# Attention 0 of a two-layer encoder: the norm's squares on ScalarE, the guard read from the matmul's bank, norm factors and outputs issued later

## The chip, the cores and the metric

The kernel runs on one core of a Trainium2 chip. A core has TensorE (PE in the profile, with its weight loads as PEld), VectorE (DVE), ScalarE (ACT) and GpSimd (POOL), and SyncE (SP), which here issues the transfers. Each engine takes its instructions in one fixed order. The time is device microseconds of one execution. Three runs of the kernel before gave 1396.01, 1396.46 and 1397.87 us: the median is 1396.46.

## The reference

Two layers over 1024 tokens of width 1024, in float32. Layer 0 is differential attention with 8 heads; layer 1 is latent attention. What matters here is layer 0:

```python
q = _rope(q.reshape(b, s, 2 * DA_HEADS, DA_QK_DIM), positions)
k = _rope(k.reshape(b, s, 2 * DA_HEADS, DA_QK_DIM), positions)
...
sc = jnp.einsum('bqhcd,bkhcd->bhcqk', qb, k) * scale
p = jax.nn.softmax(sc, axis=-1)
p = p[:, :, 0] - lam * p[:, :, 1]
o = jnp.einsum('bhqk,bkhd->bqhd', p, v)
...
o = _rmsnorm(o, subln_g) * (1.0 - lambda_init)
o = o.reshape(b, s, DA_WIDTH) * jax.nn.silu(z)
return o @ w_out
```

Every head has two softmaxes; their difference multiplies the values, and each token's 128 outputs of a head are divided by their root mean square (plus 1e-6), multiplied by a gain and by a gate silu(z).

## The kernel before, in words

**Tiles.** Attention 0 goes head by head (8), each in 8 tiles of 128 queries, four tiles to a half head. `q_tile` (line 856) computes both score matrices of a tile (128 x 1024 each, matmuls L866), the two softmaxes without their division (L412 the maximum, L414 the exponential with its sum: the first sum goes into a column of `zz`), and combines them (L872 to L874). The sums of the first softmax are not divided out: the norm that follows removes any factor of a row, so only its small added constant needs them. One and two tiles later the combined matrix is transposed (L395), split into high and low parts (L397 on ScalarE, L398 on VectorE) and multiplied by the values (`pv`, L173 to L175).

**Between them** TensorE works on strips of the input projection for the next head (`stream0`, lines 272 and 312): k, q and z. Their results go through the rotation (`rope`, line 324: L331 or L333 on ScalarE, four transfers L335, L336, L341 and L343 on POOL) and are stacked into high and low operands: `stack_q` (line 361) has two copies on ScalarE (L364, L365), two subtractions on POOL (L366, L367), and four transfers (L369, L370) that fill the other halves of qa and qb. The scores of the next head read these.

**The norm of a half head.** When the last tile of a half has been multiplied, `close` (line 1027) calls `head_out` (L931 squares the output, L932 scales it) and `subln` (line 934), which multiplies by the gate on POOL (L938) and puts `rest` on the list `hooks`. `rest` (line 942) sums the squares over the 128 partitions with small matmuls (L945) into `pt`, four columns of a bank. Then `zz` is squared (L948), the small constant times that square is added to the sum (L949), the guard compares (L950: a row whose sum of squares is too large for float32 gets a factor of 0), the sum is limited (L951), POOL raises it to the power -0.5 (L169) and multiplies by the guard (L953). `finish` (line 902) writes the 512 factors to memory (L420), reads them back spread over all partitions (L422), multiplies the output by them on POOL (L908) and stores it (L912).

**Order.** `after_scores` (line 1008) copies the list `hooks` before the second half of `pv`, and runs the copied entries after it, in each tile. So a hook that puts another on the list runs one tile earlier than that one. In numbers of tiles within a head, the gate multiply L938 of the first half is in tile 5 and that of the second half in tile 1 of the next head; `rest` is in tiles 6 and 2.

Instructions are traced in this order, and a scheduler then orders each engine by a simulation: an instruction may be issued ahead of its place when its inputs are ready. Two things pin it. `in_turn` (line 184) puts an instruction behind the one traced before it on its engine; L938, L953, L908, the rotation's and the stacks' POOL instructions and most other POOL work are pinned so, L169 is not. `tc.keep_in_program_order` does the same for some transfers of the last head; `tc.issue_after` puts one instruction behind a given one.

**The last head** has its own parts: `rest` of its first half is run by `extra0` (line 1293), which also loads and splits operands of the output projection (L1198 on ScalarE, L1199 on POOL or VectorE) and starts that projection (`Pre7`). For this half `pt` is four columns of an accumulator of `Pre7`. `run_tails` (line 993) finishes the last two tiles, the hooks left are run, and the stored first half of head 7 is read back (line 1385). The second half of head 7 goes another way (`dst` is given): its factors are spread by matmuls (L922, L923).

Of the kernel before, what the change touches and what calls it, by code (L numbers as in the profile page):

```python
# [11 lines left out]
F32 = mybir.dt.float32  # L12
# [3 lines left out]
AF = mybir.ActivationFunctionType  # L16
ALU = mybir.AluOpType
# [4 lines left out]
P = 128  # L22
# [4 lines left out]
HF = 512  # L27
NH = 8
QL = 384
KVL = 256  # L30
EPS = 1e-6
# [38 lines left out]
GUARD = 2.0 ** 40  # L70
FMAX = 3.4028e38
# [5 lines left out]
def f32v(ap):  # L77
    return ap.bitcast(F32)
# [3 lines left out]
def trunk(ctx: ExitStack, tc: tile.TileContext, A, out):  # L82
    nc = tc.nc
    SP, PE, V, S, G = nc.sync, nc.tensor, nc.vector, nc.scalar, nc.gpsimd

    def pool(stack, name, bufs=1, side="left", space=None):
        kw = dict(name=name, bufs=bufs, reuse_waits="tile")
        if space is not None:
            kw["space"] = space
            if space == DRAM:  # L90
                kw.pop("reuse_waits")
        else:
            kw["side"] = side
        return stack.enter_context(tc.tile_pool(**kw))
# [21 lines left out]
    def bank(tag, name, shape=None):  # L116
        nonlocal turn
        if tag == "acc":
            turn += 1
            if (turn - 1) % (2 + NB.get("accx", 0)) < 2:  # L120
                return psa.tile([P, HF], F32, name=name, tag="acc", bufs=2)
            tag = "accx"
        return ps.tile(shape or [P, HF], F32, name=name, tag=tag, bufs=NB[tag])

    dr = pool(ctx, "dr", bufs=1, space=DRAM)
# [6 lines left out]
    oF = [dr.tile([NH, 2, P, HF], F32, name=f"oF{l}") for l in range(2)]  # L132
# [33 lines left out]
    def rsqrt(w, n):  # L166

        y = sm.tile([P, n], F32, name="rq_y")
        G.tensor_tensor(out=y, in0=w, in1=mhalf[:, :n], op=ALU.pow)  # L169
        return y  # L170
# [9 lines left out]
    def behind(eng):  # L180

        return tc.issue_after(mk[eng]) if eng in mk else nullcontext()

    def in_turn(ins):

        return tc.keep_in_program_order(ins) if mk else ins
# [230 lines left out]
    def bcast_rows(sp, y, tag, bufs):  # L417

        d_ = dr.tile([HF], F32, name="bc_d", tag="bcd", bufs=4)
        SP.dma_start(d_.rearrange("(p t) -> p t", p=P), y)  # L420
        b = sp.tile([P, HF], F32, name="bc_s", tag=tag, bufs=bufs)
        SP.dma_start(b, d_[None, :].to_broadcast([P, HF]))  # L422
        return b, b.rearrange("p (q t) -> p t q", t=4)

    def t3(ap_):
        return ap_.rearrange("p (t q) -> p t q", t=4)
# [173 lines left out]
    for f in range(2):  # L600
        fs = slice(f * HF, f * HF + HF)
        spread = PE.matmul(cb[:, fs], ones[0:1, :], crow[0:1, fs], start=True, stop=True).ins
# [298 lines left out]

    def finish(o, y, l, h, half, dst, ap_, dgs):

        if dst is None:
            b, rb = bcast_rows(ap_, y, "osq", 4)

            def scale():
                in_turn(G.tensor_mul(t3(o), t3(o), rb))  # L908
                hooks.append(lambda: hooks.append(store))

            def store():
                SP.dma_start(oF[l][h, half], o)  # L912

            if l == 0 and (h, half) >= (NH - 2, 1):
                hooks.append(lambda: hooks.append(scale))
            else:
                hooks.append(scale)
            return
        rb = bank("z", "rb") if l else Y[1]
        for j in range(4):  # L920
            js = slice(j * P, (j + 1) * P)
            S.mul(dgs[:, js], ident, y[:, j : j + 1])  # L922
            PE.matmul(rb[:, js], ones, dgs[:, js], start=True, stop=True)  # L923
        V.tensor_mul(o, o, rb)
# [9 lines left out]
    def subln(o, sq, zz, half, h, dst):  # L934


        if dst is None:
            in_turn(G.tensor_mul(o, o, GZ[h][half]))  # L938
        else:
            V.tensor_mul(o, o, GZ[h][half])  # L940

        def rest():
            pt = Y[0] if dst is not None else ssq_at[0] if ssq_at else bank("acc", "ssq")
            for j in range(4):
                PE.matmul(pt[:, j : j + 1], sq[:, j * P : (j + 1) * P], ones[:, 0:1], start=True, stop=True)  # L945
            w = sm.tile([P, 4], F32, name="sl_w")
            fin = sm.tile([P, 4], F32, name="sl_f")
            V.tensor_mul(fin, zz, zz)  # L948
            V.scalar_tensor_tensor(out=w, in0=fin, scalar=P * EPS / GUARD ** 2, in1=pt[:, 0:4], op0=ALU.mult, op1=ALU.add)  # L949
            V.scalar_tensor_tensor(out=fin, in0=fin, scalar=FMAX / GUARD ** 2, in1=w, op0=ALU.mult, op1=ALU.is_ge)  # L950
            V.tensor_scalar(w, w, 3.0e38, None, op0=ALU.min)  # L951
            y = rsqrt(w, 4)
            in_turn(G.tensor_mul(y, y, fin))  # L953
            if dst is not None:
                return lambda: finish(o, y, 0, h, half, dst, None, sq)
            finish(o, y, 0, h, half, None, a0b, sq)

        if dst is None:
            (hooks if h < NH - 1 else rests).append(rest)
        else:  # L960
            return rest()
# [29 lines left out]
    tails, hooks = [None, None], []  # L991
# [171 lines left out]
    class Seven:  # L1163
# [32 lines left out]
        def put(self, raw, hi, lo, eng):  # L1196
            with behind("S"):
                S.copy(hi, raw)  # L1198
            sub = eng.tensor_sub(lo, raw, f32v(hi))  # L1199
            if eng is G:  # L1200
                in_turn(sub)
                self.sub = sub.ins
# [204 lines left out]
    def strip1(i, wpool=None):  # L1407
        return load_strip([A["w_s1"][i, f] for f in range(2)], [4, 4], wpool)
# [377 lines left out]
    for h in range(2):  # L1786
        w = strip1(6 + h)
# [286 lines left out]
    def attn1(h, fills, extra=None, late=None):  # L2074
# [5 lines left out]
        def close(half, o_, zz):  # L2080
            if late and half == 1:
                ctx_["late"] = late(o_, zz, ctx_["gz"])
                return
            o = ap2.tile([P, HF], F32, name="o1", tag="o", bufs=2)
            V.scalar_tensor_tensor(out=o, in0=o_, scalar=0.5, in1=ctx_["gz"], op0=ALU.mult, op1=ALU.mult)
            V.reciprocal(zz, zz)
            finish(o, zz, 1, h, half, None, ap2, None)
# [188 lines left out]
    def scale(tt, y):  # L2276
        full, early = xs_[tt], tt // 4
        c1, c2_ = halves[early], halves[1 - early]

        def second():  # L2280
            V.scalar_tensor_tensor(out=full[:, c2_], in0=full[:, c2_], scalar=y, in1=fg[:, c2_], op0=ALU.mult, op1=ALU.mult)
            SP.dma_start(out[tt][:, c2_], full[:, c2_])

        def first_():
            S.mul(full[:, c1], full[:, c1], y)
            SP.dma_start(out[tt][:, c1], full[:, c1])

        if tt == NT - 2:
            held.extend((second, first_))
        else:  # L2290
            second()
            first_()
# [160 lines left out]
```

## Time and profile before

| | |
|---|---|
| median of three runs | 1396.46 us |
| the profiled execution's own time | 1394.95 us |
| its span | 1393.2 us |
| TensorE busy | 1367.5 us (98%) |
| VectorE busy | 928.3 us (67%) |
| GpSimd busy | 753.1 us (54%) |
| ScalarE busy | 740.9 us (53%) |
| attention 0 | about 140 to 690 us of the span |

Instructions are named by their line: L908 is line 908. A group's row gives the operation, the tile written and the tiles read, the shapes, the count, then busy time in us, the mean of one in ns, and the idle time of its engine just before with what ended it. A row of the timeline gives the start and the duration in us, and in brackets the idle time before it with its releaser. In the rows of waits stand who waited, for whom, the total in us, how often, and the longest. Matmuls overlap, so their rows in the timeline run longer than the step from one to the next.

### The profile page before, as it was taken

Reading aid. Unit: us, or ns where it says so; the run is one execution under the profiler, and the core shown is the slowest. Engines: PE = TensorE matmul, PEld = TensorE weight load, DVE = VectorE, ACT = ScalarE, POOL = GpSimd, SP = SyncE. Lnnn points to the kernel's source line nnn. Section 1 sums busy time; section 2 is a strip of 40 time slices with the busy share of each in tenths; the row PEclk is TensorE's granted clock in tenths of the full one; section 3 lists DMA queues with packets and bytes.
Section 4 is the critical chain, followed back from the end, with each engine's and each line's share of the span. In section 5 each row is a group of like instructions: output and inputs, shape, how many; then the busy total and the mean of one; then the engine's idle time right before and its main releaser. Section 6 shows DMA issues by size and latency. Waiting matters only on the chain.

```text
span 1393.2 us, 20695 instructions
## 1 busy us (share of the span) xinstructions
PE 1367.5 (98%) x7334; PEld 1144.7 (82%) x7334; DVE 928.3 (67%) x1313; ACT 740.9 (53%) x1339; POOL 753.1 (54%) x593
## 2 busy tenths in 40 slices
PE   9999999999999999999999999999999999999997
PEld 6788888888888887887887888888888888888886
DVE  7655777777666666668596976545656555555684
ACT  5532465656565555567648553335454544545554
POOL 5424374758686858575794233532141373834673
PEclk9999999999999999999999999999999999999999
DMA  9857644343444434526564246489443364667463
GB/s 342 263 177 244 201 110 141 100 144 105 149 127 144 128 121 122 151 61 212 182 219 167 68 137 212 137 282 286 125 105 119 102 201 136 193 221 215 145 245 121
DMA packets 149386, 232.06 MB, mean 167 GB/s; under 512 B 20641, under 2 KB 57633, under 8 KB 149282
## 3 DMA queue, kind: packets, MB, share of 16 engines
q1 hardware_dynamic: 149282, 230.74, 52.7%
q8 instruction: 58, 0.95, 0.3%
q14 instruction: 46, 0.38, 0.1%
HBM read 144.74 MB, written 61.81 MB: 148 GB/s over the span
## 4 chain that ended last, share of the span: by engine, by line
PE 79%; DVE 6%; DMA 5%; ACT 3%; POOL 3%; issue 2%; SPq 1%; POOLq 0%; ACTq 0%; DVEq 0%
PE s L2067 10%; PE acc L173 9%; PE acc L175 9%; PE acc L174 9%; PE tr L395 7%; PE s L866 7%; PE pv L173 4%; PE pv L174 4%; PE pv L175 4%; PE vps L173 2%; PE vps L174 1%; PE vps L175 1%; PE zacc L175 1%; PE zacc L173 1%; PE zacc L174 1%
## 5 line engine op out<-in xcount | busy, mean ns | idle before, releaser
L397 ACT CAST pth<-tr 128x512 fp32r<-128x512 f32 x256 | 150.3, 587 | 285.7 <-PE tr L395 280.8
L412 DVE TENSOR_REDUCE nm<-s 128x1 f32<-128x1024 f32 x192 | 233.8, 1218 | 79.8 <-PE s L866 70.9
L398 DVE TENSOR_TENSOR ptl<-tr,pth 128x512 fp32r<-128x512 f32 x256 | 176.1, 688 | 150.3 <-ACT pth L397 146.3
L219 POOL TENSOR_TENSOR wl<-wraw,wh 128x512 fp32r<-128x512 f32 (+2 forms) x77 | 98.8, 1284 | 208.4 <-ACT wh L218 176.3
L414 ACT ACTIVATE e<-s,nm 128x1024 f32<-128x1024 f32 x128 | 143.5, 1121 | 35.4 <-DVE nm L412 35.0
L395 PE MATMUL tr<-ident,e 128*128 128x128 f32 x1024 | 155.0, 273 | 4.1 <-DVE ptl L398 3.8
L395 PEld LDWEIGHTS tr<-ident,e 128*128 128x128 f32 x1024 | 120.7, 140 | 46.5 <-DVE ptl L398 24.1
L173 PE MATMUL acc<-h0h,wh 128*128 128x512 f32 x360 | 150.2, 417 | 0.0
L173 PE MATMUL pv<-pth,vt 128*128 128x256 f32 x512 | 147.5, 288 | 0.0
L174 PE MATMUL pv<-ptl,vt 128*128 128x256 f32 x512 | 145.6, 284 | 0.0
L175 PE MATMUL pv<-pth,vt 128*128 128x256 f32 x512 | 144.6, 282 | 0.0
L175 PE MATMUL acc<-h0h,wl 128*128 128x512 f32 x360 | 141.5, 393 | 0.0
L174 PE MATMUL acc<-h0l,wh 128*128 128x512 f32 x360 | 141.1, 392 | 0.0
L336 POOL TENSOR_TENSOR rp_r<-rp_raw,cosT 128x512 f32<-128x512 f32 x36 | 47.0, 1305 | 104.4 <-ACT rp_raw L333 52.9
L173 PEld LDWEIGHTS pv<-pth,vt 128*128 128x128 f32 x512 | 97.2, 190 | 2.9 <-ACT pth L397 0.2
L174 PEld LDWEIGHTS pv<-ptl,vt 128*128 128x128 f32 x512 | 97.4, 190 | 2.4
L175 PEld LDWEIGHTS pv<-pth,vt 128*128 128x128 f32 x512 | 97.3, 190 | 0.0
L1199 POOL TENSOR_TENSOR wol<-wol,woh 128x512 fp32r<-128x512 f32 x56 | 82.3, 1492 | 26.0 <-ACT woh L1198 24.4
L866 PE MATMUL s<-ks,qa 128*128 128x512 f32 x256 | 82.7, 403 | 4.4 <-DVE e L874 3.2
L874 DVE SCALAR_TENSOR_TENSOR e<-s,z,e 128x1024 f32<-128x1024 f32 x64 | 82.2, 1284 | 2.2
L866 PE MATMUL s<-ks,qb 128*128 128x512 f32 x256 | 79.8, 393 | 1.2 <-DMA qb<-qb 1.2
L175 PEld LDWEIGHTS acc<-h0h,wl 128*128 128x128 f32 x360 | 67.6, 188 | 15.1
(427 smaller groups left out, 3461.1 us busy)
## 6 DMA issues: line engine op xcount, KB each, us to landing
ada<-in_ada_ss SPq DMA_DIRECT2D x32, 512.0 KB, 5.9
wraw<-in_w_s SPq DMA_DIRECT2D x64, 256.0 KB, 2.8
vS<-v_hl SPq DMA_DIRECT2D x32, 512.0 KB, 5.9
vt<-vS SPq DMA_DIRECT2D x32, 512.0 KB, 4.9
wol<-tS SPq DMA_DIRECT2D x56, 256.0 KB, 5.2
tS<-ob SPq DMA_DIRECT2D x48, 256.0 KB, 2.0
rp_sw<-rp_raw SPq DMA_DIRECT2D x160, 64.0 KB, 2.0
bc_s<-bc_d SPq DMA_DIRECT2D x34, 256.0 KB, 4.2
```

What stands on the lines that cost most here:

```text
L173: PE.matmul(psum, ah, bh, start=first, stop=False, skip_group_check=skip)
L174: PE.matmul(psum, ah, bl, start=False, stop=False, skip_group_check=skip)
L175: mm3.last = PE.matmul(psum, al, bh, start=False, stop=last, skip_group_check=skip).ins
L219: sub = (V if pair_of else G).tensor_sub(l_[:, :n], raw[:, :n], f32v(h_[:, :n]))
L395: transpose_p.last = PE.transpose(tr[:, j, :], p[:, kt * P : (kt + 1) * P], ident).ins
L397: mk["S"] = S.copy(pth[kh][:, :, dst], tr).ins
L398: mk["V"] = V.tensor_sub(ptl[kh][:, :, dst], tr, f32v(pth[kh][:, :, dst])).ins
L412: mk["V"] = V.reduce_max(nm, s_ps, axis=AX.X, negate=True).ins
L414: mk["S"] = S.activation(e, s_ps, AF.Exp, bias=nm, scale=1.0, accum_out=zs).ins
L866: PE.matmul(s_ps[:, kc * HF : (kc + 1) * HF], src[:, c, ql], KS[h][kc][:, c, :], start=fst, stop=not fst)
L1199: sub = eng.tensor_sub(lo, raw, f32v(hi))
L2067: PE.matmul(s_ps[:, kc * HF : (kc + 1) * HF], lhs, rhs(kc), start=i == 0, stop=i == 4)
```

## The change

Three parts. The squares of `zz` are made by two ScalarE activations, one scaled for the small constant and one for the guard. VectorE then has two instructions instead of four: one limits the sum in the bank and adds the first square, the other compares the second square with the sum in the bank, which before was compared with the sum with its small constant. And `finish` for the halves of layer 0 that go through memory no longer issues the write, the read back, the multiply and the store from `rest` on, but each from a hook of its own: with `rest` in tile t, the write of the factors goes from t to t+1, the read back from t to t+2, the multiply from t+1 to t+3 (for the two late halves of heads 6 and 7 from t+2), the store from t+3 to t+4. The multiply stays pinned by `in_turn`. Layer 1 keeps its order.

```diff
     def finish(o, y, l, h, half, dst, ap_, dgs):
 
+        if dst is None and l == 0:
+            d_ = dr.tile([HF], F32, name="bc_d", tag="bcd", bufs=4)
+            rb = []
+
+            def put():
+                SP.dma_start(d_.rearrange("(p t) -> p t", p=P), y)
+                hooks.append(spread)
+
+            def spread():
+                b = ap_.tile([P, HF], F32, name="bc_s", tag="osq", bufs=4)
+                SP.dma_start(b, d_[None, :].to_broadcast([P, HF]))
+                rb.append(b.rearrange("p (q t) -> p t q", t=4))
+                hooks.append(scale)
+
+            def scale():
+                in_turn(G.tensor_mul(t3(o), t3(o), rb[0]))
+                hooks.append(store)
+
+            def store():
+                SP.dma_start(oF[l][h, half], o)
+
+            hooks.append(put)
+            return
         if dst is None:
             b, rb = bcast_rows(ap_, y, "osq", 4)
 
...
-            if l == 0 and (h, half) >= (NH - 2, 1):
-                hooks.append(lambda: hooks.append(scale))
-            else:
-                hooks.append(scale)
+            hooks.append(scale)
             return
...
-            V.tensor_mul(fin, zz, zz)
-            V.scalar_tensor_tensor(out=w, in0=fin, scalar=P * EPS / GUARD ** 2, in1=pt[:, 0:4], op0=ALU.mult, op1=ALU.add)
-            V.scalar_tensor_tensor(out=fin, in0=fin, scalar=FMAX / GUARD ** 2, in1=w, op0=ALU.mult, op1=ALU.is_ge)
-            V.tensor_scalar(w, w, 3.0e38, None, op0=ALU.min)
+            S.activation(w, zz, AF.Square, scale=math.sqrt(P * EPS) / GUARD)
+            S.activation(fin, zz, AF.Square, scale=1.0 / GUARD)
+            V.scalar_tensor_tensor(out=w, in0=pt[:, 0:4], scalar=3.0e38, in1=w, op0=ALU.min, op1=ALU.add)
+            V.scalar_tensor_tensor(out=fin, in0=fin, scalar=FMAX, in1=pt[:, 0:4], op0=ALU.mult, op1=ALU.is_ge)
             y = rsqrt(w, 4)
             in_turn(G.tensor_mul(y, y, fin))
```

## The prediction

> **What bounds the kernel now.** I read the page first, then the busy time by stretch, who TensorE waits for, and the instructions of each engine in order of time where TensorE waits.
>
> ```profile
> span 1393.2 us, 20695 instructions
> ```
> ```profile
> 140.00:400.00 260.00, 259.31 (x1435) 220.27 (x1434) 194.10 (x276) 152.90 (x271) 164.33 (x131) 1.00 0.45 132
> 400.00:690.00 290.00, 281.25 (x1586) 235.69 (x1586) 198.12 (x283) 171.46 (x303) 206.69 (x171) 1.00 0.45 136
> ```
>
> The two stretches are attention 0 (columns: length, then busy time of PE, PEld, DVE, ACT, POOL, then granted clock). TensorE is idle for 0.7 us in the first and 8.8 us in the second, at full clock. So the whole stage holds 9.5 us that any edit beside TensorE could win: 0.7% of the time. Losses have no such limit. What TensorE waited for there:
>
> ```profile
> PE s L866 <- DVE e L874: 3.2, 6, 1.0
> PE tr L395 <- DVE ptl L398: 2.8, 5, 0.9
> PE s L866 <- DMA qb<-qb: 1.2, 2, 0.7
> PE s L866 <- DMA qa<-qa: 0.9, 1, 0.9
> ```
>
> Two thirds of the idle time ends with VectorE, 2.1 us with the query operands qa and qb, which POOL (L366, L367) and SP deliver for the next head.
>
> **The change part by part.**
>
> *Vector arithmetic of the norm (16 half heads).*
>
> ```profile
> L948 DVE TENSOR_TENSOR sl_f<-zz 128x4 f32<-128x4 f32 x16 | 9.0, 565 | 0.0
> ...
> L950 DVE SCALAR_TENSOR_TENSOR sl_f<-sl_f,sl_w 128x4 f32<-128x4 f32 x16 | 6.6, 413 | 0.4
> L951 DVE TENSOR_SCALAR sl_w<-sl_w 128x4 f32<-128x4 f32 x16 | 6.0, 373 | 0.0
> ```
> ```profile
> L949 DVE SCALAR_TENSOR_TENSOR sl_w<-sl_f,ssq x14: 132/157/159, 195.8 to 640.9; 128x4 f32<-128x4 f32 x14
> ```
>
> L948 and L951 go. L949 stays with other operations; L950 now takes its second input from the matmul's bank, as L949 does, so I price it like L949: 157 ns in place of 413. VectorE sheds 9.0 + 6.0 + 16 x (0.413 - 0.157) = 19.1 us. Most of this lies under TensorE's work. Where it does not, the trace shows it:
>
> ```profile
> 331.72 1.22 DVE L951 TENSOR_SCALAR sl_w<-sl_w 128x4 f32<-128x4 f32 x1
> 332.85 0.26 DVE L873 TENSOR_SCALAR z<-z,zz,neglam 128x1 f32<-128x1 f32 x1
> 333.15 1.28 DVE L874 SCALAR_TENSOR_TENSOR e<-s,z,e 128x1024 f32<-128x1024 f32 x1
> ```
> ```profile
> 334.49 0.73 PE L866 MATMUL s<-ks,qa 128*128 128x512 f32 x2 [0.59 <-DVE e L874]
> ```
>
> L951 holds up the two steps behind it, L873 and L874, and TensorE waits 0.59 us for L874. Without L951's 1.22 us that wait is gone. Upper bound of the gain: all that VectorE ends, 3.2 + 2.8 = 6.0 us; lower bound: nothing, if other VectorE work fills the place. The wait above is the one I can tie to these instructions for certain; I take a quarter of the bound, **-1.5 us**, since most of the 11 waits end a chain of full-width softmax steps (L874's 1.28 us and its like) that stay.
>
> The bank is now read twice, the second time by the guard. In the last head it is an accumulator that TensorE overwrites later; the second read is 0.16 us, so nothing to at most 16 x 0.16 = 2.5 us. I take nothing, because no wait of TensorE on L949 is among the four above.
>
> *Two squares on ScalarE.* The trace has no Square of this shape. The nearest row is a small activation:
>
> ```profile
> L843 ACT ACTIVATE lp<-lp x1: 205/205/205, 105.1 to 105.1; 128x2 f32<-128x2 f32 x1
> ```
>
> 32 x 0.205 = 6.6 us, in 550 us where ScalarE is busy 152.90 + 171.46 = 324.4. The inputs are old by then, so the squares can go into gaps. In the worst case each stands ahead of a copy that TensorE wants: +6.6 us; in the best nothing. I take **+0.2**, near the idle end.
>
> [...] L948 took 565 ns on VectorE in the mean, L843 205 ns on ScalarE. [...]
>
> *The multiply by the norm factors (L908) goes two tiles later.* Put, spread and store go one, two and one tile later; but the trace shows that work which isn't pinned is issued when its inputs are there, not at its place in the text:
>
> ```profile
> 672.65 0.92 DVE L948 TENSOR_TENSOR sl_f<-zz 128x4 f32<-128x4 f32 x1
> ...
> 688.53 0.16 DVE L949 SCALAR_TENSOR_TENSOR sl_w<-sl_f,oy 128x4 f32<-128x4 f32 x1 [0.65 <-PE oy L945]
> ```
>
> These are neighbouring lines of one half head, 16 us apart. So I cost the two transfers, which are not pinned, at nothing: the same 15 of each on SP, behind the same producers (a gain or loss of one SP slot, 0.5 us, where they trade places with a query copy). L908 is pinned behind all earlier POOL work, so it does move: from tiles 3 and 7 of each head to tiles 5 and 1, and there it stands right behind L938, the gate multiply of the next half.
>
> ```profile
> L908 POOL TENSOR_TENSOR o<-o,bc_s 128x512 f32<-128x512 f32 x15 | 23.2, 1549 | 16.9 <-DMA bc_s<-bc_d 16.8
> ```
>
> What it gains: POOL's 16.8 us of waiting for the broadcast row end, as two more tiles pass. TensorE felt this once:
>
> ```profile
> 650.52 1.55 POOL L908 TENSOR_TENSOR o<-o,bc_s 128x512 f32<-128x512 f32 x1 [5.67 <-DMA bc_s<-bc_d]
> ```
> ```profile
> 654.48 0.50 PE L175 MATMUL oy<-woh,oal 128*128 128x512 f32 x1 [0.51 <-POOL oal L1199]
> ```
>
> That is **-0.5** (bounds 0 and -0.5). What it costs: 1.55 us of POOL at tile 5, ahead of the query operands of the next head. Head 4:
>
> ```profile
> 396.81 1.29 POOL L938 TENSOR_TENSOR o<-o,gz 128x512 f32<-128x512 f32 x1
> ...
> 405.77 1.29 POOL L366 TENSOR_TENSOR qb<-rp_r,qa 64x512 fp32r<-64x512 f32 x1
> 407.14 1.29 POOL L367 TENSOR_TENSOR qb<-rp_r,qa 64x512 fp32r<-64x512 f32 x1
> ```
> ```profile
> 411.22 0.47 PE L866 MATMUL s<-ks,qb 128*128 128x512 f32 x1 [0.55 <-DMA qb<-qb]
> ```
>
> POOL never pauses between these rows, and TensorE already waits: +1.55. Head 7 and head 3, with SP's copies of qb and the matmul that reads it:
>
> ```profile
> 603.24 1.28 POOL L938 TENSOR_TENSOR o<-o,gz 128x512 f32<-128x512 f32 x1 [4.07 <-ACT o L932]
> ...
> 616.28 1.29 POOL L367 TENSOR_TENSOR qb<-rp_r,qa 64x512 fp32r<-64x512 f32 x1
> ```
> ```profile
> 338.17 0.46 SPq L370 DMA_DIRECT2D qb<-qb x1
> 617.60 0.46 SPq L370 DMA_DIRECT2D qb<-qb x1
> ```
> ```profile
> 341.43 0.62 PE L866 MATMUL s<-ks,qb 128*128 128x512 f32 x2
> 620.37 0.62 PE L866 MATMUL s<-ks,qb 128*128 128x512 f32 x2
> ```
> ```profile
> DMA to landing us min/median/max: 2.2/2.3/5.7
> ```
>
> In head 7 POOL's pause of 4.07 us ends at L938, so nothing earlier helps. With 2.2 us to landing, head 7 has 620.37 - 619.8 = 0.6 us to spare and loses 1.0; head 3 has 341.43 - 340.4 = 1.0 and loses 0.5. In heads 5 and 6 the old place of L908 lies on the same unbroken stretch of POOL, so its going there pays for its coming:
>
> ```profile
> 518.07 1.57 POOL L908 TENSOR_TENSOR o<-o,bc_s 128x512 f32<-128x512 f32 x1
> ```
>
> I take 0 for these. Sum **+3.0**; bounds 0 and 5 x 1.55 = 7.75.
>
> *Last head.* L908 of head 6's second half comes behind the last L938 and ahead of a weight split that TensorE wants at once:
>
> ```profile
> 664.39 1.27 POOL L1199 TENSOR_TENSOR wol<-wol,woh 128x512 fp32r<-128x512 f32 x1
> ```
> ```profile
> 665.85 0.39 PE L174 MATMUL oy<-wol,oah 128*128 128x512 f32 x1
> ```
>
> It ends at 665.66, 0.19 us early, so 1.55 more makes up to 1.36 us of wait; I take **+1.0**, as VectorE paces what follows (bounds 0 and 1.4). The last L908 leaves its place before the splits and comes behind them; the store and reload of that row move some 4 us later on SP, where the loads behind them have over 8 us to spare. In the very last half, which the output projection waits for, POOL's power no longer follows L950 and L951, 0.41 + 0.37 us by their means: **-0.5**, as these steps are shorter where POOL is quiet; bounds 0 and -0.8.
>
> Sum: -1.5 + 0.2 - 0.5 + 3.0 + 1.0 - 0.5 = **+1.7 us**. The profiled execution took 1394.95 us, 1.75 outside its span; it becomes 1396.65. The median of the runs shown is 1.51 above it, so **1398.2 us**.
>
> **The rivals.**
>
> *POOL decides (slower).* L908 behind L938 delays the query operands of all five heads 3 to 7, 7.75 us, and the last head's split, 1.4; less 1.5, 0.5 and 0.5 that is +6.65, or 1403.1 us. It holds from the point where a head has less than 1.55 us to spare and POOL no pause between L938 and L367; three heads are shown to be so. Against it: in heads 5 and 6 L908 leaves the same stretch, and faster vector work lets POOL start earlier.
>
> *VectorE decides (faster).* If short vector work ends all its 6.0 us, and the two 0.5 with it, while L908 falls into pauses, the time is 1396.46 - 7.0 = 1389.5; half of this gives 1393.0. For it: the waits are VectorE's, by two thirds. Against it: L874, L412 and L398 stay as they are.
>
> *The squares decide (slower).* If each of the 32 stands ahead of a copy that TensorE wants, the term is 6.6 in place of 0.2, and the time 1404.6. For it: ScalarE's copies lie in TensorE's own loop. Against it: ScalarE has pauses for 41% of the stage, and the squares' inputs are two tiles old.
>
> *The moves don't take place in effect.* If POOL's order comes out as before, since what is pinned is pinned behind other work that itself waits, only the arithmetic counts: -1.5 + 0.2 - 0.5 = -1.8, or 1394.7 us.
>
> **How the numbers follow.** Forecast 0.32, POOL decides 0.29, the squares decide 0.03, VectorE decides 0.24, no moves in effect 0.12. About 0.2% (2.8 us) is what a measurement of this kernel tells from no change. The forecast and the third rival lie within it: 0.44. Slower 0.32, faster 0.24. The likeliest one's own range is 1394.5 to 1400.5. The range over all goes to 1391.5, where about a third of the faster case is left out, and to 1403, where the last part of the slower one is: about 0.16 outside.
>
> **What would show it.** Right: L908 directly behind L938 on POOL, with no wait for bc_s; L366 and L367 of heads 3, 4 and 7 later against the head's L938 by 1.5 us, and longer waits of the first score matmul of a head on qa and qb; the guard near 0.16 us in every half; the wait at 334.49 gone; squares of about 0.2 us on ScalarE. Wrong: waits on qa and qb no longer than now (then POOL has more room than I read), TensorE idle in attention 0 well under 8 us, or a new wait on pth behind the squares.

## The result, and the profile after

The changed kernel takes 1403.91 us (median of six runs, 1400.24 to 1405.51) where the kernel before takes 1396.36: a ratio of 1.0048, 95% interval 1.0032 to 1.0064. It is slower, by 7 us, and 0.9 us beyond the upper end of the range.

The profiled execution was the fastest of the six. Its own time is 1400.24 us. The first two rows of its page:

```profile
span 1398.5 us, 20660 instructions
...
PE 1366.8 (98%) x7334; PEld 1145.4 (82%) x7334; DVE 914.6 (65%) x1281; ACT 745.3 (53%) x1371; POOL 753.5 (54%) x593
```

VectorE is busy 13.7 us less than before (928.3), TensorE about as long as before (1367.5). The own times of the norm's instructions, four before and two now, fell by 19.2 us (24.1 to 4.9), as the prediction summed them; the busy time fell less: 6.1 us of the 24.1 overlapped neighbouring VectorE instructions before, and 2.8 of the 4.9 do now, which makes 3.3 of the 5.5 us between the two. The span grew by 5.3 us, so TensorE's idle time grew by 5.3 + 0.7 = 6.0 us. The two stretches of attention 0 (columns as in the prediction) hold 4.0 of these; another 2.0 lie ahead of 140 us, where TensorE's idle time ranges from 4.6 to 8.5 us over the profiles of all kernels here.

```profile
140.00:400.00 260.00, 260.00 (x1442) 221.40 (x1440) 188.22 (x263) 155.71 (x287) 166.92 (x133) 1.00 0.45 132
400.00:690.00 290.00, 276.56 (x1557) 232.37 (x1557) 187.55 (x262) 172.83 (x320) 198.77 (x165) 0.99 0.43 131
```

From 140 to 400 us TensorE has no idle time left: the wait at 334.49 is gone. From 400 to 690 us idle time has grown from 8.8 to 13.4 us. Whom TensorE waited for in attention 0 (140 to 700 us):

```profile
PE tr L395 <- DVE ptl L398: 7.8, 7, 2.6
PE s L866 <- DVE e L874: 1.9, 2, 1.2
PE oy L174 <- POOL wol L1219: 1.3, 1, 1.3
PE oy L173 <- ACT oah L1218: 1.1, 1, 1.1
PE oy L175 <- POOL oal L1219: 0.6, 1, 0.6
PE s L866 <- DMA qb<-qb: 0.3, 1, 0.3
```

The waits on qa and qb, which the prediction saw grow, have shrunk from 2.1 to 0.3 us. What has grown is the transpose's wait on ptl, from 2.8 to 7.8 us, and three waits in the last head are new. (Lines behind `finish` are 20 higher than before: L938 is now L958, L945 L965, L1199 L1219. L908 is now L919.)

**The stall ahead of head 5** (as in the prediction, a place is named by the head whose queries are being made) in the timeline of the changed kernel, engine by engine:

```profile
463.47 1.31 POOL L958 TENSOR_TENSOR o<-o,gz 128x512 f32<-128x512 f32 x1
464.71 1.56 POOL L919 TENSOR_TENSOR o<-o,bc_s 128x512 f32<-128x512 f32 x1
...
470.08 1.29 POOL L343 TENSOR_TENSOR rp_r<-rp_r,rp_sw 128x512 f32<-128x512 f32 x1
471.40 0.62 ACT L364 CAST qa<-rp_r 64x512 fp32r<-64x512 f32 x1 [3.81 <-POOL rp_r L343]
...
473.18 0.58 ACT L397 CAST pth<-tr 128x512 fp32r<-128x512 f32 x1
473.79 0.69 DVE L398 TENSOR_TENSOR ptl<-tr,pth 128x512 fp32r<-128x512 f32 x1 [3.16 <-ACT pth L397]
474.54 0.66 PE L395 MATMUL tr<-ident,e 128*128 128x128 f32 x4 [2.56 <-DVE ptl L398]
```

The same place in the kernel before, whose rows the prediction did not show:

```profile
465.53 1.30 POOL L938 TENSOR_TENSOR o<-o,gz 128x512 f32<-128x512 f32 x1
...
470.64 1.29 POOL L343 TENSOR_TENSOR rp_r<-rp_r,rp_sw 128x512 f32<-128x512 f32 x1
471.96 0.62 ACT L364 CAST qa<-rp_r 64x512 fp32r<-64x512 f32 x1 [2.23 <-POOL rp_r L343]
475.10 0.66 PE L395 MATMUL tr<-ident,e 128*128 128x128 f32 x4 [0.87 <-DVE ptl L398]
```

The multiply stands where the prediction put it, directly behind the gate multiply (ahead of heads 6 and 7 with three instructions and one between), and it never waits for bc_s. But its 1.56 us lie ahead of L343, the last step of the rotation of the next head's queries, and L343's first consumer is not GpSimd's own L366 but a copy on **ScalarE**, L364. ScalarE takes its instructions in order: while L364 waits 3.81 us (2.23 before), the copy L397 of a transposed tile, whose input is ready (its transposes end at 469.68), waits behind it until 473.18 (L365 and L333 come between the two), then VectorE's L398, then TensorE's next transpose. Ahead of heads 6 and 7 the same chain costs 1.30 and 2.02 us of TensorE's time. With the 2.56 that is 5.9 us, against 0.87 + 0 + 0.40 before.

**The last head.** Two stalls are new. L919 ahead of the weight split, as predicted, 1.26 us; and the stored first half of head 7, which is read back for the output projection:

```profile
669.64 0.50 PE L174 MATMUL oy<-wol,oah 128*128 128x512 f32 x1 [1.26 <-POOL wol L1219]
...
683.23 0.32 SPq L923 DMA_DIRECT2D oF<-o  x1
685.22 0.32 SPq L1405 DMA_DIRECT2D k<-oF  x1
...
687.85 0.62 ACT L1218 CAST oah<-k 128x512 fp32r<-128x512 f32 x1 [3.92 <-DMA k<-oF]
...
688.52 0.50 PE L173 MATMUL oy<-woh,oah 128*128 128x512 f32 x1 [1.08 <-ACT oah L1218]
```

Before, the store was issued at 676.34 and the read back at 678.40; both are now 6.8 to 6.9 us later. Of these, 3.7 us are the delay of the whole kernel up to there (the last score matmul starts at 674.38 in place of 670.73); the order itself makes 3.2. Before, ScalarE copied the row at 681.36 without a wait for it; now it waits 3.92 us, again with its other work behind that.

### The profile page after: what moved, and what is told of

Read it like the earlier page. It is cut to its first block, busy times and chain, and to the rows that moved or that the text cites. A ratio compares the mean times of both kernels' runs of the same rounds, so it can differ in the third digit from the quotient of the medians.

```text
span 1398.5 us, 20660 instructions
## 1 busy us (share of the span) xinstructions
PE 1366.8 (98%) x7334; PEld 1145.4 (82%) x7334; DVE 914.6 (65%) x1281; ACT 745.3 (53%) x1371; POOL 753.5 (54%) x593
## 4 chain that ended last, share of the span: by engine, by line
PE 77%; DVE 6%; POOL 5%; DMA 4%; ACT 4%; issue 3%; SPq 1%; POOLq 0%; ACTq 0%; DVEq 0%
PE s L2087 10%; PE acc L173 8%; PE acc L175 8%; PE acc L174 8%; PE tr L395 7%; PE s L866 6%; PE pv L173 4%; PE pv L174 4%; PE pv L175 4%; PE vps L173 1%; PE vps L175 1%; PE vps L174 1%; PE zacc L175 1%; PE zacc L174 1%; PE zacc L173 1%
## 5 line engine op out<-in xcount | busy, mean ns | idle before, releaser
L397 ACT CAST pth<-tr 128x512 fp32r<-128x512 f32 x256 | 150.3, 587 | 284.8 <-PE tr L395 281.3
L398 DVE TENSOR_TENSOR ptl<-tr,pth 128x512 fp32r<-128x512 f32 x256 | 176.3, 689 | 161.9 <-ACT pth L397 157.7
L1219 POOL TENSOR_TENSOR wol<-wol,woh 128x512 fp32r<-128x512 f32 x56 | 82.4, 1494 | 30.3 <-ACT woh L1218 24.8
L874 DVE SCALAR_TENSOR_TENSOR e<-s,z,e 128x1024 f32<-128x1024 f32 x64 | 82.2, 1284 | 2.2
```

What stands on the lines that cost most here:

```text
L397: mk["S"] = S.copy(pth[kh][:, :, dst], tr).ins
L398: mk["V"] = V.tensor_sub(ptl[kh][:, :, dst], tr, f32v(pth[kh][:, :, dst])).ins
```

## Experiments

The ratios below are against the kernel before on the same chip, with 95% intervals. One thousandth is 1.4 us.

| kernel | median us | ratio |
|---|---|---|
| changed kernel | 1403.91 | 1.0048 [1.0032, 1.0064] |
| the same again | 1402.88 | 1.0043 [1.0031, 1.0056] |
| moves only | 1403.76 | 1.0053 [1.0041, 1.0065] |
| arithmetic only | 1395.52 | 0.9991 [0.9982, 0.9999] |
| changed, both late halves old | 1400.12 | 1.0022 [1.0013, 1.0032] |
| changed, second half of head 6 old | 1400.83 | 1.0036 [1.0023, 1.0049] |

**Arithmetic only, moves only.** `arith_only` is the kernel before with the new four lines of `rest`; `moves_only` the changed kernel with the old four.

> The kernel before with the new vector arithmetic alone (two squares on ScalarE, two VectorE instructions); the norm's multiply, put, spread and store stay where they were. Theory A (the loss comes from where the multiply by the norm factors now stands on GpSimd, and the arithmetic is a gain): faster than before by 2 to 3 us, about 1393.8 us, with no wait of TensorE near 334.5 and 411 us. Rival S (the two squares on ScalarE delay the copies that TensorE wants): slower than before, up to 1403 us, and the wait of the transpose on ptl stays at 2 us and more in heads 5 to 7.

> The changed kernel with the old four VectorE instructions: only the moves of put, spread, multiply and store. Theory A: slower than the changed kernel by the 2 to 3 us that the arithmetic saves, about 1406 us, and ScalarE's first copy of the query stack (L364) still waits over 2.5 us for L343 in heads 5 and 7. Rival S: at 1397 us, since the squares are gone.

The arithmetic wins 1.3 us, less than the 2 to 3 expected; the moves alone cost 7 us (2 us less than the 1406 expected), with ScalarE waiting 3.74 and 3.78 us for L343 ahead of heads 5 and 7, as expected of theory A. There TensorE waits only 1.06 and 0.56 us on ptl, because it has already waited 1.16 and 1.15 us just before, on L874 behind the old limiting of the sum (1.22 us each time); the sums, 2.22 and 1.71 us, are near the 2.56 and 2.02 of the changed kernel. Rival S fails in both: without moves the squares do not make the kernel slower, and without the squares it is as slow. Beside the moves, the arithmetic's part is 0.7 to 1.4 us by the ratios (1.0053 less 1.0048 or 1.0043), and within the intervals it may be nothing.

**Where the arithmetic's gain went.** In `arith_only` the wait at 334.49 is gone, but a new one stands in head 7:

```profile
674.58 0.62 ACT L1198 CAST oah<-oal 128x512 fp32r<-128x512 f32 x1 [2.59 <-DMA oal<-oF]
675.10 1.08 ACT L414 ACTIVATE s<-s,nm 128x1024 f32<-128x1024 f32 x1
...
677.35 0.50 PE L173 MATMUL oy<-woh,oah 128*128 128x512 f32 x1 [2.18 <-ACT p L1286]
```

The scheduler, with other instructions to place, put a copy that waits 2.59 us for its load ahead of the exponential of the last tile; before, the exponential came first. `arith_but_head7` has the new four lines under the first branch and the old four under the second, which is taken for both halves of head 7:

```diff
+            if dst is None and not ssq_at:
...
+            else:
...
```

> The kernel before with the new vector arithmetic in heads 0 to 6 only; both halves of head 7 keep the four VectorE instructions. Theory O (the arithmetic gains about 2 us in heads 1 to 6, and loses them in head 7 because ScalarE's order changes there: a copy that waits for its load stands ahead of the exponential of the last tile): the wait of 2.18 us in front of L173 at 677 us vanishes, and the time falls by about 2 us against arith_only, to 1393.5 us. Rival S (two more ScalarE squares per half cost by themselves): two halves of 16 less, so a change of 0.1 us at most against arith_only, 1395.4 us.

Measured: 1393.97 us, 0.9984 [0.9975, 0.9993]; ScalarE's order in head 7 is that of before, and the wait of 2.18 us is gone. Theory O holds. Whether it is the squares' presence on ScalarE or VectorE's shorter times that tip the scheduler's order was not separated. Since part of the arithmetic's gain was open, it was run once more:

> arith_but_head7 once more, beside vector_but_head7 and the kernel before on one chip. If the gain of the arithmetic without its loss in head 7 is real, 2 to 2.5 us below the kernel before; if it was this kernel's luck on the first chip, within 1 us of it.

1393.86 us, 0.9982 [0.9974, 0.9991]: the gain is real, 2.2 to 2.5 us.

**The last head apart.** `tail_old` gives the late halves their old order, `tail61_old` only the second half of head 6:

```diff
-        if dst is None and l == 0:
+        if dst is None and l == 0 and (h, half) < (NH - 2, 1):
```

> The changed kernel, but the second half of head 6 and the first half of head 7 are finished in the old order; all other halves as changed. Theory T (a part of the loss lies in the last head: the weight split behind the multiply, and the stored row of head 7 that is read back later): the waits of 1.26, 1.08 and 0.62 us at 669 to 690 us vanish, 3 us faster than the changed kernel, about 1401 us. Theory A alone: the last head's stalls are hidden by later waits, and the time stays within 1 us of the changed kernel.

> The changed kernel with the old order for the second half of head 6 alone, whose multiply stands ahead of the weight split; the first half of head 7 stays as changed, with its stored row read back later. Theory T: of the 3.8 us that tail_old won, the split's wait (1.26 us at 669.6) goes and the waits of 1.08 and 0.62 us at 688 to 690 us stay: 1401.5 to 1402.5 us. Rival: one of the two halves carries all of it: 1400 or 1404 us.

`tail_old` is 3.8 us faster than the changed kernel by the medians and 2.9 to 3.6 by the ratios; `tail61_old` 3.1 by its median, a little under the time expected, though by the ratios only 1.0 to 1.7. In the trace of `tail61_old` the split's wait is gone and those on oah and oal at 688 us stay (1.24 and 0.62 us). In `tail_old` all three are gone, but the reordered copy of `arith_only` is there: it waits 2.32 us for its load, and TensorE 1.91 us at 682 us. So what the late halves cost is seen less that stall. By the ratios it is 1.0 to 1.7 us for the multiply ahead of the split and 2.0 us for the row that is read back late; the intervals overlap, so how the cost divides between the two is not shown. What is left of the moves, up to the first half of head 6, is the difference between `tail_old` and `arith_only`: 0.0031, or 4.3 us, about the 4.6 us of idle time that heads 5 to 7 gained.

**Is it GpSimd's time ahead of L343?** First, the multiply one tile later, behind the L343 of the first half:

```diff
-                hooks.append(scale)
+                hooks.append(scale if (h, half) >= (NH - 2, 1) else lambda: hooks.append(scale))
```

> The changed kernel with the multiply by the norm factors one tile later again for all halves up to the first of head 6, so that GpSimd does it behind L343 of the next head's queries and not ahead of it; the two late halves stay as changed. Theory A: ScalarE's wait in front of L364 in heads 5 to 7 falls by about 1.5 us each, TensorE's waits of 2.56, 1.30 and 2.02 us on ptl there fall to 0.5 or less each, and the time falls by 4 to 5 us, to about 1399.5 us. Rival Q (the prediction's step: the second operands L366 and L367 come late): the multiply still stands ahead of L366 and L367, so waits on qb in heads 5 to 7 and the time stay, 1403 to 1405 us.

```profile
469.47 0.62 ACT L364 CAST qa<-rp_r 64x512 fp32r<-64x512 f32 x1 [2.26 <-POOL rp_r L343]
472.61 0.66 PE L395 MATMUL tr<-ident,e 128*128 128x128 f32 x4 [0.96 <-DVE ptl L398]
...
485.47 0.62 ACT L364 CAST qa<-rp_r 64x512 fp32r<-64x512 f32 x1 [3.57 <-POOL rp_r L343]
488.81 0.88 PE L395 MATMUL tr<-ident,e 128*128 128x128 f32 x4 [2.22 <-DVE ptl L398]
```

In the place that it left, the wait of L364 is back at 2.26 us and TensorE's at 0.96. But the multiply, in tile 6, now stands ahead of the L343 of the second half, and there the same chain appears; ahead of heads 6 and 7 it costs TensorE 1.79 and 2.20 us. The time, 1401.98 us (1.0046), hardly moves: the expected 4 to 5 us were won in one place and lost in the other. The stall follows the multiply. Rival Q's long waits on qb did not come (0.4 us in all).

Second, the cost without the move. `extra_op` is `arith_but_head7`, nothing moved, plus one GpSimd instruction of 1.29 us behind the gate multiply (it changes no value):

```diff
             in_turn(G.tensor_mul(o, o, GZ[h][half]))
+            if half == 0 and 4 <= h <= 6:
+                o4 = o.rearrange("p (q t) -> p q t", t=P)
+                in_turn(G.tensor_mul(o4, o4, ones[:, None, :].to_broadcast([P, 4, P])))
```

> arith_but_head7 (nothing moved) with one more GpSimd instruction, a multiplication of the same tile by ones, right behind the gate multiply of the first half in heads 4, 5 and 6; all transfers and the norm's multiply stay in their old places. Theory A (1.3 to 1.55 us of GpSimd ahead of L343 is the whole cause in heads 5 to 7): ScalarE waits 1.3 to 1.5 us longer in front of L364 there, TensorE's waits on ptl in heads 5 to 7 grow to 2.5, 1.3 and 2.0 us, and the time rises by 3.5 to 5 us, to 1397.5 to 1399 us. Rival M (the other moves, of put, spread and store on SyncE, cost the time in these heads): within 1 us of arith_but_head7, 1394 us.

```profile
473.53 0.62 ACT L364 CAST qa<-rp_r 64x512 fp32r<-64x512 f32 x1 [3.62 <-POOL rp_r L343]
...
476.67 1.11 PE L395 MATMUL tr<-ident,e 128*128 128x128 f32 x4 [2.38 <-DVE ptl L398]
...
547.52 0.66 PE L395 MATMUL tr<-ident,e 128*128 128x128 f32 x4 [1.18 <-DVE ptl L398]
...
618.38 0.65 PE L395 MATMUL tr<-ident,e 128*128 128x128 f32 x4 [1.86 <-DVE ptl L398]
```

1399.5 us, 1.0015 [1.0006, 1.0024], that is 4.3 us above `arith_but_head7` by the ratios, and half a microsecond over the range expected. Three instructions with 3.9 us in all reproduce the three stalls of the changed kernel (5.4 us in all, 1.4 without them), and rival M falls.

Third, the move without the cost. `scale_on_vector` is `tail_old` with the multiply on VectorE, in the changed kernel's tiles:

```diff
-                in_turn(G.tensor_mul(t3(o), t3(o), rb[0]))
+                with behind("V"):
+                    V.tensor_mul(t3(o), t3(o), rb[0])
```

> tail_old with the multiply by the norm factors done by VectorE instead of GpSimd, in the same tiles, for the halves that are in the new order. Theory A: GpSimd has lost the 1.55 us ahead of L343, ScalarE's waits in front of L364 fall to about 2.2, 1.2 and 2.2 us, TensorE's waits on ptl in heads 5 to 7 to 0.9, 0.4 and 0.5 us, and the time falls by 3 to 4.5 us against tail_old, to 1396 us. Rival V (VectorE, with 0.7 us more per half in the softmax loop, takes its place as the one that TensorE waits for): 1399 us and more, with waits on e (L874) of over 0.5 us in several heads.

1395.99 us, 0.9995 [0.9986, 1.0004]: 3.8 us faster than `tail_old`. The waits on ptl in heads 6 and 7 are 0.5 us and less; in head 5 1.72 us stay, which the expectation had at 0.9: L364 still waits 3.03 us there. The multiply took VectorE 1.35 us in the mean, not 0.7, and VectorE's own waits hold TensorE 2.5 us where `tail_old` had 1.6; rival V is a small part at most. Theory A holds in all three, with the rest in head 5 left open.

**Is the block on ScalarE the whole chain?** `copies_later` is `tail_old` with the stack's copies later in ScalarE's order in heads 6 and 7, so that L397 goes ahead of them:

```diff
-*[None] * (DEF - 1 - ROT - (h == NH - 1)), *sum_, g)
+*[None] * (DEF - 1 - ROT - (h == NH - 1) + 2 * (h > 4 and half == 0)), *sum_, g)
```

> tail_old, with the stacking of the first half's queries (L364 to L370) traced two strip steps later in heads 5 to 7, which puts ScalarE's copies L364 and L365 behind one more copy of a transposed tile (L397) in heads 6 and 7, and behind none more in head 5; the place of the norm's multiply on GpSimd stays. Theory A (a copy that waits for GpSimd holds up the copy of the transposed tile behind it on ScalarE): TensorE's waits on ptl of 1.25 us at 548 and 2.02 us at 618 us fall under 0.6 us, that of 2.52 us at 476 us stays, and the time falls by 2.5 to 4 us against tail_old, to 1396 to 1397.6 us. Rival Q (the query operands' own lateness): the waits move to qa and qb at the heads' first scores, and the time stays at 1400 us or rises.

TensorE's waits in that kernel, 140 to 700 us:

```profile
PE s L866 <- DMA qa<-qa: 5.7, 3, 2.5
PE tr L395 <- DVE ptl L398: 3.4, 4, 2.0
```

The stalls on ptl in heads 6 and 7 are gone, and that of head 5 stays at 1.98 us, as theory A says: ScalarE's block is what makes them. But waits on qa came, 1.49, 1.68 and 2.53 us in heads 5, 6 and 7, and the time stays: 1399.9 us (1.0022), rival Q's number. The trace says where they come from; head 6:

```profile
542.43 0.62 ACT L365 CAST qa<-rp_r 64x512 fp32r<-64x512 f32 x1
544.52 2.41 SPq L335 DMA_DIRECT2D rp_sw<-rp_raw  x4
547.04 0.53 SPq L369 DMA_DIRECT2D qa<-qa  x1
549.86 0.70 PE L866 MATMUL s<-ks,qa 128*128 128x512 f32 x2 [1.68 <-DMA qa<-qa]
```

The copies into qa end at 543.05, but their first transfer is issued 4.0 us later, behind four transfers of the rotation; in `tail_old` it is issued at 546.42, ahead of them, 0.4 us after the copies end. The edit traced the transfers later too, and so made the second wait itself, also in head 5, where L397 kept its place behind the copies. The run shows the block, and does not show that the query operands would be late without it; what the time would be with the transfers in their old places stays open.

**Two more versions.** The multiply on VectorE in its old tiles, and all findings together (`scale_on_vector` with head 7 as in `arith_but_head7`):

> arith_but_head7 with the multiply by the norm factors on VectorE up to the first half of head 6, in its old tiles. Theory A: GpSimd has 1.55 us less per half, so ScalarE's waits in front of L364 become shorter than now and the time falls by up to 1 us, to 1393 to 1394 us. Rival V: the multiply waits for its broadcast row on VectorE, in front of the softmax, and the time rises to 1398 us or more.

> scale_on_vector with the four old VectorE instructions in both halves of head 7, as in arith_but_head7: the moves up to the first half of head 6, their multiply on VectorE, the new arithmetic in heads 0 to 6. Theory A with O: the wait of 1.41 us in front of L173 at 676 us vanishes, no stall over 2 us is left, and the time is 1.5 us under scale_on_vector, 1394.5 us, level with arith_but_head7. Rival: the new order of ScalarE in head 7 was no cause, and the time stays at 1396 us.

`best_vector` is the slowest of all, 1409.26 us (1.0096). In the old tiles the broadcast row is not there yet, and now VectorE waits for it, with the softmax behind; its row of waits:

```profile
DVE o L910 <- DMA bc_s<-bc_d: 19.0, 8, 5.3
```

On GpSimd such waits (16.8 us before) cost TensorE little: at most the 0.88 and 0.55 us on qa and qb at 410 us, which are gone with the moves. So the move of the multiply to later tiles does have a use: it makes the engine free to choose. `vector_but_head7` takes 1395.3 us, 0.9985 [0.9976, 0.9994], no better than `arith_but_head7` without any move. None is better than the arithmetic in heads 0 to 6 with nothing moved.

**The spread.** The first profile was 3.7 us under its kernel's median, so the changed kernel was run again:

> The changed kernel once more, unchanged. Its first profile was of its fastest run (1400.24 us of a median of 1403.9). Theory G (a stall of some 2 us on TensorE is at times followed by a stretch at half clock that costs 1.7 us more, and the start varies by 2 us): a median of 1403 to 1404.5 us, spread over 4 us and more, and a profile that shows stretches at half clock in other places than the first. Rival: the spread belongs to the first chip; all runs within 2 us.

1402.88 us, 1400.73 to 1403.55: a spread of 2.8 us, not 4, and a median just under the range expected. Its profile shows the same stalls as the first to 0.1 us (2.47, 1.24 and 2.00 us in heads 5 to 7), and the stretches at half clock in other places; more on these below.

## Why the prediction was wrong, point by point

The sign of the sum was right and its size was not: +1.7 was forecast, some 7 came. The path of the largest term was wrong, and the last head, forecast at 1.0 - 0.5 = +0.5, cost some 3 us. In the order of the steps:

- **Vector arithmetic, -1.5.** Right. By itself the arithmetic gains 1.3 us with what head 7 gives back, 2.2 to 2.5 us without. Beside the moves it is 0.7 to 1.4 us, and within the intervals perhaps nothing. The guard takes 148 ns from the bank (157 forecast), and the wait at 334.49 is gone.
- **Squares, +0.2.** They take 205 and 190 ns, as forecast, where L948 on VectorE took 565 ns in the mean, and no wait of TensorE up to head 6 ends with them. Missed: a changed instruction list changes the scheduler's order elsewhere. Head 7's new wait of 2.18 us in `arith_only` is that.

```profile
L968 ACT ACTIVATE sl_w<-zz x16: 205/205/216, 170.7 to 674.6; 128x4 f32<-128x4 f32 x16
...
L971 DVE SCALAR_TENSOR_TENSOR sl_f<-sl_f,ssq x14: 146/148/148, 196.4 to 643.1; 128x4 f32<-128x4 f32 x14
```

- **L908's own wait, -0.5.** Misread. In the kernel before, L908 ends at 652.07 and GpSimd then idles 1.08 us before the split that TensorE waits for, so its wait for bc_s was not what delayed the split. With L908 gone from there, TensorE still waits 0.51 us at this place in the second profile of the changed kernel; in the first it doesn't, but there TensorE itself runs at half clock just then.
- **L908 moved, +3.0: the step that failed.** The place, the 1.55 us and the missing wait for bc_s were right; the consumer and the heads were wrong. The step looked for who reads qa and qb (L366, L367, the transfers). It passed over L343 on the same GpSimd stretch, which releases ScalarE's L364, and over what stands behind L364 on ScalarE. What came is 4.3 us by the runs, in heads 5 to 7 (idle time 5.9 us in place of 1.3); of the heads it counted, 3, 4 and 7, only head 7 lost anything. The row of L364 in the trace before already showed waits for L343 of 2.23, 1.60 and 2.28 us in heads 5 to 7, and 2.8 us of TensorE's waits on ptl were quoted but not followed back.
- **Heads 3 and 4, +0.5 and +1.55.** Nothing came; TensorE's waits of 0.88 and 0.55 us at 410 us are even gone. "GpSimd never pauses between these rows" was true and did not suffice: the unbroken stretch itself began 3.7 us earlier (the gate multiply of head 4 at 393.08 in place of 396.81), mostly because L908 had left it with its 1.83 us of wait and 1.55 us of work at 376.25. So 1.55 us more still left L366 2.2 us early: here its going did pay for its coming.
- **Heads 5 and 6, 0.** Here the same reasoning failed the other way. "Its going pays for its coming" holds only if GpSimd can use the time that L908 frees. Ahead of head 6, where the stretch was unbroken before, GpSimd after the change waits for its suppliers between the old place and the new one:

```profile
520.13 1.29 POOL L219 TENSOR_TENSOR wl<-wraw,wh 128x512 fp32r<-128x512 f32 x1 [0.42 <-ACT wh L218]
...
525.79 1.29 POOL L341 TENSOR_TENSOR rp_sw<-rp_sw,sinT 128x512 f32<-128x512 f32 x1 [0.39 <-DMA rp_sw<-rp_raw]
...
531.49 1.31 POOL L336 TENSOR_TENSOR rp_r<-rp_raw,cosT 128x512 f32<-128x512 f32 x1 [0.53 <-ACT rp_raw L333]
533.53 1.28 POOL L958 TENSOR_TENSOR o<-o,gz 128x512 f32<-128x512 f32 x1 [0.73 <-ACT o L952]
```

  These four are 2.1 us, more than the 1.55 that was freed. Ahead of head 5 it is the same: pauses of 1.35 and 1.12 us where the kernel before had one, of 0.43 (so that stretch was not quite unbroken, as the prediction has it). Early work cannot be done before its inputs; late work is late all the same.
- **Weight split, +1.0.** The wait came, 1.26 us; by the runs 1.0 to 1.7 us, within intervals that overlap.
- **Store and reload of head 7's first half, at nothing.** Wrong, and the largest miss in size. In the kernel's own order they came 3.2 us later, near the 4 forecast, but the row itself had no time to spare: ScalarE waits 3.92 us for it and TensorE 1.08 + 0.62 us behind that. By the runs it is about 2 us, not cleanly parted from the split.
- **The last half, -0.5.** Did not come. Its two VectorE instructions end 0.23 us after the first starts, but POOL's power then stands behind another POOL instruction: it starts 2.3 us after the sum's instruction, where before it was 0.8. What that costs was not tested. That these steps are shorter where POOL is quiet shows in the trace before: L948, L950 and L951 take 0.15 to 0.17 us in the 18 cases where no POOL instruction runs beside them, and up to 1.29 us where one does; in the last half L950 and L951 took 0.31 and 0.17 us.

By its own test the prediction was wrong: "waits on qa and qb no longer than now". Its first rival, "POOL decides" at 1403.1 us, had the engine, the sign and nearly the time, but by the same wrong consumer: the loss is not 1.55 us in each of five heads but 1.3 to 1.7 us in three. That its number fits is in part luck: two heads lost nothing, and the last head lost some 3 us, which was not in that sum.

## What to carry to other kernels

When an instruction moves on one engine, follow every instruction behind it to its consumers, and then ask on each consumer's engine what stands behind the one that waits: here a copy that waited 3.81 us for GpSimd held up what came next on ScalarE. Time freed earlier in an engine's queue pays for time added later only if the work between has its inputs by then. And an edit that moves nothing can still reorder another stage through the scheduler, so look at the order of every engine, in the stage with the least slack above all.

## What the runs showed of the hardware

The granted clock was not expected to matter. In all fifteen profiles of this case it changes in steps of 3.41 us, or whole multiples of it: the stretches at half clock between 140 and 760 us are 3.41 us long each, and within a profile all start a whole number of such steps apart. By the granted clock such a stretch costs an estimated 1.7 us, half of its length; in the changed kernel's first profile 128x512 matmuls started 0.43 us apart in it (656.31 and 656.74) and 0.23 us apart at full clock (613.65 and 613.88). Two steps of the changed kernel's first profile, one behind the other, then two of its second (columns as in the prediction; the clock is the third number from the end):

```profile
650.50:653.91 3.41, 1.64 (x9) 1.00 (x8) 3.40 (x4) 1.53 (x2) 0.00 (x0) 1.00 0.98 342
653.91:657.32 3.41, 3.41 (x12) 2.54 (x10) 1.99 (x5) 3.12 (x8) 1.35 (x2) 0.50 1.05 377
...
472.73:476.14 3.41, 0.94 (x7) 0.64 (x6) 1.39 (x2) 3.30 (x8) 3.26 (x5) 1.00 0.78 246
476.14:479.55 3.41, 3.41 (x16) 3.11 (x15) 2.69 (x5) 1.75 (x5) 2.52 (x2) 0.50 0.64 174
```

Such stretches stand, between 140 and 760 us, in every profile with the stalls of GpSimd's moved multiply or of the extra instruction: one in the first profile of the changed kernel, two in the second (476 and 671 us), three in `scale_later`, two in `extra_op`. There is none in the kernel before, in `arith_only` (though that has a wait of 2.18 us), in both profiles of `arith_but_head7` and in `vector_but_head7`; `scale_on_vector` has one. Not every one stands behind a stall of the multiply: that of the first profile, at 653.91, and that of `scale_on_vector` follow a wait of 1.24 us on L874 that `arith_only` has too.

The same stall had one behind it in one profile and none in the other, and the steps fell differently on it. The stall of 2.56 us at 474 us in the first profile lies in two steps and leaves TensorE 1.87 us busy in the emptier one (473.00 to 476.41), and no stretch follows; in the second profile it lies in one step, 0.94 us busy, and one follows. Over all profiles, from 30 to 1380 us, a stretch at half clock followed only steps in which TensorE was busy 1.74 us or less, about half of the step: every time at 1.44 us and less (nine steps), six times of thirteen from 1.55 to 1.74, and never above. So a stall of TensorE of some 2 us cost at times itself and at times 1.7 us more here. That this makes up the spread of the runs is likely, but only the profiled runs show it.
